# Two rows of a layer norm's gain and bias, spread over 128 partitions by TensorE in place of a broadcasting load

## The chip, the cores and the metric

The kernel runs on one core of one Trainium2 chip. The metric is device time in microseconds (us) of one execution. Names of engines: PE is TensorE (PEld its weight loads), DVE is VectorE, ACT is ScalarE, POOL is GpSimd and SP is SyncE, which here issues the weight DMAs.

## What is computed

One transformer block on 512 tokens of width 2048, all in float32. Three mixers (a spatial gating unit, a gated recurrence and latent attention) feed an output projection; then come a layer norm, a mixture of 32 experts with two experts per token, and a second layer norm. What matters here is cut down to:

```
x = layer_norm(ALPHA * x + mix, ln1_g, ln1_b)     # x: 512 x 2048
ffn = hierarchical_moe(x, ...)                    # 32 experts, top 2 of one group of 8
    # per expert e: h = silu(xb @ w_gate[e]) * (xb @ w_up[e]);  y = h @ w_down[e]
x = layer_norm(ALPHA * x + ffn, ln2_g, ln2_b)
# layer_norm: (x - mean) * rsqrt(var + eps) * g + b, g and b of length 2048
```

## The kernel before

Tokens lie in NB = 4 blocks of 128 rows. After the output projection four tiles `z[b]` (128 x 2048) hold the first norm's result without its gain and bias. For the experts these two are applied to the gathered, transposed rows, from a small column table. For the residual of the second norm they are still to be applied to `z` itself: `z = z * g + b`, where `g` and `b` must stand in every partition, since a token is a partition.

The expert loop (`for e in range(NE)`) takes the experts one after the other. For each one, `up(e)` multiplies the gathered rows by `w_gate` and `w_up` (16 chunks of 128 x 1024, 512 KB each, through the class `Ring`), and `down(e - 1)` multiplies the previous expert's hidden rows by `w_down` (8 chunks). A chunk is loaded by SP into a raw buffer (line 81), then split into a high and a low part by ACT (line 96, copy to fp32r) and DVE (line 97, subtract) into one of four pairs of buffers, and TensorE multiplies the parts (lines 1390 and 1391 in `up` where an expert has at most 64 rows, lines 156 to 158 in `down` and in `up` of larger experts). Chunks of two of the four column parts of `down` aren't split: there TensorE multiplies in plain float32 (line 1426). `Ring.done()` hands a used buffer back and pumps the next load and split. Each engine works its instructions in the order in which the program writes them, so what is written between `up(e)` and `down(e - 1)` stands there on every engine's queue.

PSUM tiles come from two rings: `acc()` with five buffers and `aux()` with three. `rows` turns the gathered rows with TensorE through `aux` (line 1348) for the next expert, `fold` and `turn_h` (lines 1400, 1407, and the split at 161 and 162) make the hidden rows of `down`.

Between `up(12)` and `down(11)` the helper `vectors` loads `ln1_g` and `ln1_b` into two tiles of 128 x 2048 (tags X7 and B2): SP issues two DMAs whose source is read 128 times, 1 MB each (line 1526). In the experts 13 to 28, between `up(e)` and `down(e - 1)`, DVE applies a quarter of one block per expert, a multiply and an add of 128 x 512 (line 1566). After the last `up`, `vectors` loads the second norm's vectors in the same way into tiles of the same tags.

Of the kernel before, what the change touches and what calls it, by code (L numbers as in the profile page):

```python
# [13 lines left out]
AF = mybir.ActivationFunctionType  # L14
# [9 lines left out]
DM = 2048  # L24
# [105 lines left out]
def build(tc, I, out):  # L130
    with ExitStack() as ctx:
        _build(tc, tc.nc, ctx, I, out)


def _build(tc, nc, ctx, I, out):
# [8 lines left out]
    def slot(tag, shape, dt=F32):  # L144
        cnt[0] += 1
        return bp.tile([P] + list(shape), dt, tag=tag, name=f"{tag}_{cnt[0]}")
# [4 lines left out]
    mm = nc.tensor.matmul  # L151
    tt, ts, stt = nc.vector.tensor_tensor, nc.vector.tensor_scalar, nc.vector.scalar_tensor_tensor
    act = nc.scalar.activation
# [73 lines left out]
    for k2 in range(8):  # L227
        t = slot(f"X{k2}", [2, 2, 512], F32R)
# [19 lines left out]
    ones = onesr.bitcast(F32)  # L248
# [28 lines left out]
    def bcast(ap, n):  # L277
        return bass.AP(tensor=ap.tensor, offset=ap.offset, ap=[[0, P], [1, n]])
# [39 lines left out]
    def acc(shape=(512,)):  # L318
        return ps.tile([P] + list(shape), F32, tag="acc", name="acc", bufs=5)

    def aux(shape=(512,)):
        return ps.tile([P] + list(shape), F32, tag="aux", name="aux", bufs=3)

    def btile():
        o = acc()
        for half in range(2):
            w = ring.get()
            for j in range(8):
                k = half * 8 + j
                c = slice(j * P, (j + 1) * P)  # L330
                mm3(o, (w[0][:, c], w[1][:, c]), xk(k), k == 0, k == KD - 1)
            ring.done()
            step()
        return o
# [114 lines left out]
    for h in range(4):  # L449
        o = btile()  # L450
# [347 lines left out]
    o = aux()  # L798
# [36 lines left out]
    def pv(h):  # L835
        o = acc()
        for s in range(NB):
            v = [x[:, s, (h % 4) * P:(h % 4 + 1) * P] for x in V[h // 4]]
            pt = [x[:, POFF[s]:POFF[s] + T - P * s] for x in ptk]
            mm3(o[:, s * P:], v, pt, s == 0, s == NB - 1)  # L840
        return o
# [55 lines left out]
    for h in range(7):  # L897
# [16 lines left out]
        o = pv(h)  # L914
# [35 lines left out]
    o = pv(7)  # L950
# [13 lines left out]
    gb1 = [slot("X7", [DM]), slot("B2", [DM])]  # L964
# [209 lines left out]
    for b in range(NB):  # L1174
        o = acc()
# [107 lines left out]
    def gates():  # L1283
        tt(gv, oh, wide(gate, [2 * NB, NE], 2), op=OP.mult)
        hl = tp[:, 0:512].rearrange("p (i a e) -> p i a e", a=2, e=NE)
        yield
        act(hl[:, :, 0], gv, AF.Copy)
        tt(hl[:, :, 1], gv, hl[:, :, 0].bitcast(F32), op=OP.subtract)
        yield
        o = aux()  # L1290
        for i in range(2 * NB):
            mm(o[:, 0:2 * NE], ohr[:, i // NB, i % NB], hl[:, i].rearrange("p a e -> p (a e)"),
               start=i == 0, stop=i == 2 * NB - 1)
        nc.vector.tensor_copy(gt, o[:, 0:NE])
        tt(gt, gt, o[:, NE:2 * NE], op=OP.add)
        yield
# [25 lines left out]
    def gather(e):  # L1322
        def move(n):
            for i in range(2):
                nc.gpsimd.indirect_dma_start(out=xgs[e % 2][0:n, H[i]], out_offset=None, in_=x1d[i][:],  # L1325
                                             in_offset=off(idx[0:n, EX[e]:EX[e] + 1]),
                                             bounds_check=T - 1, oob_is_err=False)
        if e:
            sized(e, move)
        else:  # L1330

            move(32)
            with tc.If(nc.gpsimd.value_load(cnt_i[0:1, EX[0]:EX[0] + 1]) > 32):
                move(P)
# [20 lines left out]
    def rows(e, i, *by):  # L1355

        n = 4 // len(by)
        tmp = xgs[e % 2][:, i * 512:(i + 1) * 512]
        for h, ts in enumerate(by):
            o = turn(xgs[e % 2], i, range(h * n, h * n + n))  # L1360
            for j in range(h * n, h * n + n):
                g, b = [gcol[:, a, 4 * i + j:4 * i + j + 1] for a in range(2)]
                s = slice(j * P, (j + 1) * P)
                ts(tmp[:, s], o[:, s], g, b, op0=OP.mult, op1=OP.add)
        def parts():
            d = [xT[i // 2][:, 4 * (i % 2):4 * (i % 2) + 4, :, a] for a in range(2)]
            split(d[0], d[1], tmp.rearrange("p (a t) -> p a t", t=P))
        return parts

    def up(e, hooks):  # L1370


        n = nc.tensor.value_load(cnt_i[0:1, EX[e]:EX[e] + 1])
        stt(folds[e % 2], pairs, few[:, EX[e]:EX[e] + 1], ident, op0=OP.mult, op1=OP.add)
        for which in range(2):
            o = acc()
            for c in range(8):
                if (which, c) in hooks:
                    hooks[which, c]()
                if (which, c) == (1, 2):  # L1380
                    act(raws[0], fold(e, 0), AF.Silu)
                w = ring.get()
                ks = [(2 * c + j, [v[:, j * 512:(j + 1) * 512] for v in w]) for j in range(2)]
                with tc.If(n > HALF) as more:
                    for k, wk in ks:
                        mm3(o, [xT[k // 8][:, k % 8, :, a] for a in range(2)], wk, k == 0, k == KD - 1)
                with more.Else():
                    for k, wk in ks:
                        x = xT[k // 8][:, k % 8, 0:HALF].rearrange("p t a -> p (t a)")
                        mm(o, x, wk[0], start=k == 0, stop=False)  # L1390
                        mm(o, x, wk[1], start=False, stop=k == KD - 1)  # L1391
                if c == 7:
                    act(raws[which], o, AF.Copy)
                ring.done()
# [10 lines left out]
    def turn_h(e):  # L1405
        hi, lo = [v.rearrange("p a t -> p (a t)") for v in hTs[e % 2]]
        tt(hfs[e % 2], raws[0], fold(e, 1), op=OP.mult)
        split(hi, lo, hfs[e % 2])
# [30 lines left out]
    def steps_of(e):  # L1439

        steps = {}
        for i in range(4):
            steps[(0, 2 * i + 1) if e > 1 else [(0, 5), (0, 6), (0, 7), (1, 1)][i]] = lambda i=i: later.append(rows(e, i, ts, gain_act))
            steps[1, 2 * i + 2] = lambda: later.pop(0)()
        return steps
# [73 lines left out]
    later = []  # L1519
    ring.done()  # L1520

    def vectors(*names):

        ts = [slot("X7", [DM]), slot("B2", [DM])]
        for t, name in zip(ts, names):
            nc.sync.dma_start(t, bcast(I[name], DM))
        return ts

    for e in range(NE):
        if e and e + 2 < NE:  # L1530
            gather(e + 2)
        hooks = steps_of(e + 1) if e + 1 < NE else {}
        if e == 0:
            rows(0, 1, gain_act)()
            hooks[0, 0] = lambda: later.append(rows(0, 2, ts, gain_act))

            def part3():
                later.pop()()
                later.append(rows(0, 3, ts, gain_act))
            hooks[0, 2] = part3  # L1540

            def last():
                later.pop()()
                gather(2)
            hooks[0, 4] = last
            gate_table = gates()
            for c in (0, 5, 7):
                hooks[1, c] = lambda: next(gate_table)
        if e == 1:
            hooks[0, 2] = lambda: turn_h(0)  # L1550
        up(e, hooks)
        while later:
            later.pop(0)()
        if e == 9:
            for entry in lent:
                entry[1] = True
        if e == NE - 3:
            for entry in ers:
                entry[1] = True
        if e == 12:  # L1560
            gb1 = vectors("ln1_g", "ln1_b")
        if 13 <= e < 29:

            b, s = (e - 13) // 4, slice((e - 13) % 4 * 512, ((e - 13) % 4 + 1) * 512)
            for t, op in zip(gb1, (OP.mult, OP.add)):
                tt(z[b][:, s], z[b][:, s], t[:, s], op=op)
        if e == 0:
            x4 = slot("X4", [2, 1024])
            ring.add([x4[:, 0, :]])
            hfs += [x4[:, 1, i * DE:(i + 1) * DE] for i in range(2)]  # L1570
            ring.add([misc[:, 1024:]])
            ring.pump()
        elif e < NE - 1:
            down(e - 1)
    down(NE - 2)
    lng2, lnb2 = vectors("ln2_g", "ln2_b")
    down(NE - 1)

# [151 lines left out]
```

## Time and profile before

| | us |
|---|---|
| median of 3 runs | 1927.43 (1927.27 to 1928.93) |
| the profiled execution: its own time | 1928.39 |
| its span from the first to the last instruction | 1926.6 |
| DVE busy in the span | 1415.2 (73%) |
| ACT busy in the span | 1258.6 (65%) |
| PE busy in the span (matmuls are pipelined and their ends modelled) | 1815.6 (94%) |

The expert loop fills the time from about 770 us to the end. A share of the whole span mixes it with the mixers ahead, so the loop is read from rows of its own stretches. Weight loads on PEld show best when TensorE moves on: each matmul is preceded by one, and the spacing of their starts is the pace of TensorE.

### The profile page before, as it was taken

The numbers are of one execution on the slowest core, as the hardware profiler recorded it, in microseconds if no ns is written. First come the engines' busy times: TensorE is split into PE (matmuls) and PEld (weight loads), VectorE is DVE, ScalarE is ACT, GpSimd is POOL, SyncE is SP. The second block draws the span as 40 slices with busy tenths as digits, with TensorE's granted clock in tenths as the row PEclk, the third lists the DMA queues.
The fourth block names the chain that finished last, engine by engine and source line by source line (L and its number), as shares of the span: only waits on it lengthen the run. The fifth ranks groups of instructions, "written<-read, shape, count | busy, mean of one in ns | idle before, by whom it ended". The sixth has DMA issues, their size and how long they took to land.

```text
span 1926.6 us, 25404 instructions
## 1 busy us (share of the span) xinstructions
PE 1815.6 (94%) x8235; PEld 1366.7 (71%) x8236; DVE 1415.2 (73%) x2041; ACT 1258.6 (65%) x1758; POOL 242.0 (13%) x192
## 2 busy tenths in 40 slices
PE   9999999999999997899999999999999999999990
PEld 7888888887887896666666666666766666667650
DVE  5656433467564446988989889898898998988866
ACT  4533363635452224888878888787887878878862
POOL 1000000010000001112112121211212212121010
PEclk9999999999999997999999999999999999999995
DMA  7222222223145225899999999999999999999895
GB/s 252 98 88 77 77 68 97 98 88 131 44 166 193 92 82 193 290 352 381 391 392 383 390 337 393 395 378 390 383 364 395 392 393 378 381 388 385 294 348 184
DMA packets 142574, 510.78 MB, mean 265 GB/s; under 512 B 18625, under 2 KB 18673, under 8 KB 141361
## 3 DMA queue, kind: packets, MB, share of 16 engines
q1 hardware_dynamic: 131040, 477.16, 65.9%
q0 software_dynamic: 10768, 29.74, 5.7%
q8 instruction: 93, 1.52, 0.3%
q10 hardware_dynamic: 576, 1.57, 0.2%
q14 instruction: 97, 0.79, 0.1%
HBM read 488.53 MB, written 22.02 MB: 265 GB/s over the span
## 4 chain that ended last, share of the span: by engine, by line
issue 48%; POOL 5%; DMA 2%; DVE 2%; POOLq 1%; ACT 0%; PE 0%; DVEq 0%; ACTq 0%
POOL yd L1338 2%; DMA yd<-M,idx 2%; POOL M L1325 2%; POOL B L1325 2%; POOLq L1310 1%; DVE B L1620 0%; DVE X L1616 0%; POOLq L1316 0%; DVE whl L97 0%; DMA X<-w_up 0%; DVE B L1625 0%; DMA B<-yd 0%; ACT whl L96 0%; DVE B L162 0%; POOLq L1338 0%
## 5 line engine op out<-in xcount | busy, mean ns | idle before, releaser
L97 DVE TENSOR_TENSOR whl<-X,whl 128x1024 fp32r<-128x1024 f32 x312 | 377.5, 1221 | 97.4 <-ACT whl L96 67.8
L97 DVE TENSOR_TENSOR whl<-wraw,whl 128x1024 fp32r<-128x1024 f32 (+1 forms) x222 | 269.8, 1218 | 226.6 <-ACT whl L96 211.8
L96 ACT ACTIVATE whl<-wraw 128x1024 fp32r<-128x1024 f32 (+1 forms) x222 | 235.0, 1062 | 220.6 <-PE acc L157 94.0
L96 ACT ACTIVATE whl<-X 128x1024 fp32r<-128x1024 f32 x312 | 330.2, 1072 | 61.2 <-PE acc L158 39.6
L1391 PE MATMUL acc<-whl,B 128*128 128x512 f32 x696 | 287.0, 412 | 15.4 <-DVE whl L97 15.3
L1390 PE MATMUL acc<-whl,B 128*128 128x512 f32 x696 | 293.4, 421 | 2.1 <-ACT whl L96 1.7
L1338 POOL DMA_INDIRECT yd<-M,idx x64 | 90.4, 1412 | 871.6 <-ACT M L1430 866.1
L1391 PEld LDWEIGHTS acc<-whl,B 128*128 128x128 f32 x696 | 131.2, 188 | 86.7 <-DVE whl L97 59.5
L158 PE MATMUL acc<-whl,B 128*128 128x512 f32 (+1 forms) x480 | 181.4, 378 | 0.0
L157 PE MATMUL acc<-whl,B 128*128 128x512 f32 (+1 forms) x424 | 165.8, 391 | 14.6 <-DVE whl L97 14.6
L156 PE MATMUL acc<-whl,B 128*128 128x512 f32 (+1 forms) x424 | 179.2, 423 | 0.1
L1390 PEld LDWEIGHTS acc<-whl,B 128*128 128x128 f32 x696 | 131.3, 189 | 32.0 <-issue 4.8
L156 PE MATMUL acc<-X,whl 128*128 128x512 f32 x384 | 151.0, 393 | 0.0
L157 PE MATMUL acc<-X,whl 128*128 128x512 f32 x384 | 149.6, 390 | 0.3 <-DVE X L162 0.3
L158 PE MATMUL acc<-X,whl 128*128 128x512 f32 x384 | 149.6, 390 | 0.0
L1426 PE MATMUL acc<-X,X 128*128 128x512 f32 x308 | 141.2, 592 | 0.0
L97 DVE TENSOR_TENSOR X<-X,X 128x1024 fp32r<-128x1024 f32 x105 | 128.1, 1220 | 17.2 <-ACT X L96 12.9
L96 ACT ACTIVATE X<-X 128x1024 fp32r<-128x1024 f32 x105 | 112.4, 1070 | 19.8 <-PE acc L158 14.9
L1430 ACT ACTIVATE M<-acc,X 128x512 f32<-128x512 f32 x128 | 87.2, 681 | 50.3 <-PE acc L1426 43.7
L157 PEld LDWEIGHTS acc<-whl,B 128*128 128x128 f32 x424 | 80.5, 190 | 47.7 <-DVE whl L97 26.9
L1391 PE MATMUL acc<-X,B 128*128 128x512 f32 x232 | 97.8, 421 | 10.0 <-DVE X L97 9.9
L158 PEld LDWEIGHTS acc<-whl,B 128*128 128x128 f32 x480 | 90.9, 189 | 15.7
(451 smaller groups left out, 3596.0 us busy)
## 6 DMA issues: line engine op xcount, KB each, us to landing
X<-w_down SPq DMA_DIRECT2D x169, 512.0 KB
X<-w_gate SPq DMA_DIRECT2D x160, 512.0 KB
X<-w_up SPq DMA_DIRECT2D x160, 512.0 KB
wraw<-w_gate SPq DMA_DIRECT2D x69, 512.0 KB
wraw<-w_up SPq DMA_DIRECT2D x69, 512.0 KB
wraw<-w_in SPq DMA_DIRECT2D x64, 512.0 KB
wraw<-w_down SPq DMA_DIRECT2D x64, 512.0 KB
B<-w_up SPq DMA_DIRECT2D x27, 512.0 KB
```

The costliest lines, as they stand in the source:

```text
L96: nc.scalar.activation(h[:, s], r[:, s], AF.Copy)
L97: nc.vector.tensor_tensor(l[:, s], r[:, s], h[:, s].bitcast(F32), op=OP.subtract)
L156: mm(o, a[0], b[0], start=start, stop=False)
L157: mm(o, a[0], b[1], start=False, stop=False)
L158: mm(o, a[1], b[0], start=False, stop=stop)
L1310: n = nc.gpsimd.value_load(cnt_i[0:1, EX[e]:EX[e] + 1])
L1325: nc.gpsimd.indirect_dma_start(out=xgs[e % 2][0:n, H[i]], out_offset=None, in_=x1d[i][:], in_offset=off(idx[0:n, EX[e]:EX[e] + 1]), bounds ...
L1338: nc.gpsimd.indirect_dma_start(out=yd[i][:], out_offset=off(index), in_=y[:, H[i]], in_offset=None, bounds_check=T - 1, oob_is_err=False, ...
L1390: mm(o, x, wk[0], start=k == 0, stop=False)
L1391: mm(o, x, wk[1], start=False, stop=k == KD - 1)
L1426: mm(o, hfs[e % 2][:, k * P:(k + 1) * P], w[:, cs], start=k == 0, stop=k == 3)
L1430: act(yts[-1][:, n * 512:(n + 1) * 512], o, AF.Copy, scale=gt[:, EX[e]:EX[e] + 1])
```

## The change

The load of `ln1_g` and `ln1_b` between `up(12)` and `down(11)` becomes two DMAs of one row each (1 x 2048, 8 KB) into partition 0 of the same tiles. In the experts 13 and 14, between `up(e)` and `down(e - 1)`, a new helper `spread` makes each quarter of the tiles whole: a float32 matmul of a row of ones (1 x 128) with a quarter row (1 x 512) gives 128 equal rows in an `aux` tile, and ACT copies them into the tile. Each of the two experts does four of these: two quarters of each vector. The 16 pairs of DVE operations on `z` move two experts later, to the experts 15 to 30. The second norm's vectors are loaded as before.

```
+    def spread(t, q):
+
+        o, s = aux(), slice(q * 512, (q + 1) * 512)
+        mm(o, ones[0:1], t[0:1, s], start=True, stop=True)
+        act(t[:, s], o, AF.Copy)
...
         if e == 12:
-            gb1 = vectors("ln1_g", "ln1_b")
-        if 13 <= e < 29:
-
-            b, s = (e - 13) // 4, slice((e - 13) % 4 * 512, ((e - 13) % 4 + 1) * 512)
+            gb1 = [slot("X7", [DM]), slot("B2", [DM])]
+            for t, name in zip(gb1, ("ln1_g", "ln1_b")):
+                nc.sync.dma_start(t[0:1], I[name])
+        if 13 <= e < 15:
+            for q in (2 * e - 26, 2 * e - 25):
+                for t in gb1:
+                    spread(t, q)
+        if 15 <= e < 31:
+
+            b, s = (e - 15) // 4, slice((e - 15) % 4 * 512, ((e - 15) % 4 + 1) * 512)
             for t, op in zip(gb1, (OP.mult, OP.add)):
                 tt(z[b][:, s], z[b][:, s], t[:, s], op=op)
```

On TensorE, at the end of `up(13)` (whl is a split chunk, X_119 and B_120 are the two vectors' tiles):

```order
 L1391 MATMUL acc<-whl,B_116_6158 128x512
 L1384 UNCONDITIONAL_BRANCH
+L1525 MATMUL aux<-X_119_12008,onesr 128x512
+L1525 MATMUL aux<-B_120_12009,onesr 128x512
+L1525 MATMUL aux<-X_119_12008,onesr 128x512
+L1525 MATMUL aux<-B_120_12009,onesr 128x512
 L156 MATMUL acc<-whl,B_111_5475 128x512
 L157 MATMUL acc<-whl,B_111_5475 128x512
```

Four matmuls stand between the last one of `up(13)` and the first one of `down(12)`; the same four stand once more behind `up(14)`.

On ACT, at the same place (whl and X_96 are halves of chunk pairs, M_118 is a result of `down`):

```order
 L96 ACTIVATE whl<-B_106_5386 128x1024
 L161 ACTIVATE B_116_6158<-M_108_5395 128x512
+L1526 ACTIVATE X_119_12008<-aux 128x512
+L1526 ACTIVATE B_120_12009<-aux 128x512
+L1526 ACTIVATE X_119_12008<-aux 128x512
+L1526 ACTIVATE B_120_12009<-aux 128x512
 L96 ACTIVATE whl<-wraw 128x1024
 L1430 ACTIVATE M_118_6918<-acc,X_101_3986 128x512
```

The four copies stand behind two splits that were there before, the last of them line 161, and ahead of the split at line 96 with which the next chunk begins.

On SP, in the stream of weight loads behind `up(12)`:

```order
 L81 DMA wraw<-w_up 128x1024
 L81 DMA X_101_3986<-w_up 128x1024
-L1526 DMA X_119_12008<-ln_g 128x2048
-L1526 DMA B_120_12009<-ln_b 128x2048
+L1569 DMA X_119_12008<-ln_g 1x2048
+L1569 DMA B_120_12009<-ln_b 1x2048
 L81 DMA X_99_3984<-w_up 128x1024
 L81 DMA wraw<-w_up 128x1024
```

The two issues keep their place; only their size differs.

## Rows read from the trace of the kernel before

**Rows 1.** The profile page: busy time, and DMA in 40 slices.

```profile
PE 1815.6 (94%) x8235; PEld 1366.7 (71%) x8236; DVE 1415.2 (73%) x2041; ACT 1258.6 (65%) x1758; POOL 242.0 (13%) x192
...
DMA  7222222223145225899999999999999999999895
```

**Rows 2.** Busy time by stretch, one expert each, from end of down to end.

```profile
core 0: us, PE busy (x) PEld busy (x) DVE busy (x) ACT busy (x) POOL busy (x), PEclk, DMA share, GB/s
1178.30:1212.35 34.05, 32.60 (x137) 22.38 (x136) 29.49 (x36) 28.72 (x40) 6.78 (x4) 1.00 1.03 395
1212.35:1246.41 34.06, 32.62 (x138) 22.41 (x137) 30.09 (x37) 28.44 (x40) 5.83 (x4) 1.00 1.03 392
1246.41:1280.50 34.09, 32.61 (x138) 22.37 (x137) 30.79 (x37) 28.69 (x41) 6.94 (x4) 1.00 1.03 393
1280.50:1314.88 34.38, 32.90 (x138) 22.40 (x137) 30.71 (x37) 28.49 (x41) 5.97 (x4) 1.00 1.03 377
1110.17:1144.27 34.10, 32.62 (x138) 22.38 (x137) 29.50 (x36) 28.80 (x40) 6.90 (x4) 1.00 0.96 327
```

**Rows 3.** Line 1526's DMAs, then line 1566: min/median/max ns, first and last start.

```profile
L1526 SPq DMA_DIRECT2D X<-ln_g x2: 424/424/424, 1204.4 to 1868.7; - x2
...
L1566 DVE TENSOR_TENSOR B<-B,X x16: 677/688/693, 1238.6 to 1754.1; 128x512 f32<-128x512 f32 x16
```

**Rows 4.** Timeline, PEld, end of up(13), then down(12): start, us, instruction, [idle].

```profile
1232.97 0.19 PEld L156 LDWEIGHTS acc<-whl,B 128*128 128x128 f32 x1
1234.14 0.19 PEld L157 LDWEIGHTS acc<-whl,B 128*128 128x128 f32 x1 [0.98 <-DVE whl L97]
...
1237.55 0.30 PEld L1426 LDWEIGHTS acc<-wraw,X 128*128 128x128 f32 x2
1238.09 0.19 PEld L1426 LDWEIGHTS acc<-wraw,X 128*128 128x128 f32 x1 [0.24 <-issue]
...
1240.67 0.19 PEld L156 LDWEIGHTS acc<-whl,B 128*128 128x128 f32 x1 [0.24 <-issue]
...
1246.41 0.19 PEld L1426 LDWEIGHTS acc<-X,X 128*128 128x128 f32 x1 [0.24 <-issue]
```

**Rows 5.** Timeline, ACT, around the same place.

```profile
1232.45 0.71 ACT L161 ACTIVATE B<-M 128x512 fp32r<-128x512 f32 x1
1233.00 1.08 ACT L96 ACTIVATE whl<-X 128x1024 fp32r<-128x1024 f32 x1
...
1235.37 0.71 ACT L161 ACTIVATE B<-M 128x512 fp32r<-128x512 f32 x1
1236.38 1.06 ACT L96 ACTIVATE whl<-wraw 128x1024 fp32r<-128x1024 f32 x1 [0.30 <-DMA wraw<-w_gate]
```

**Rows 6.** Line 1430, ACT copies out of PSUM: min/median/max ns.

```profile
L1430 ACT ACTIVATE M<-acc,X x128: 667/687/692, 828.5 to 1883.1; 128x512 f32<-128x512 f32 x128
```

**Rows 7.** Timeline around the start of up(13): PEld, ACT, then DVE.

```profile
1213.67 0.19 PEld L1391 LDWEIGHTS acc<-whl,B 128*128 128x128 f32 x1
...
1214.38 1.06 ACT L96 ACTIVATE whl<-X 128x1024 fp32r<-128x1024 f32 x1 [0.28 <-DMA B<-ln_b]
...
1211.64 1.23 DVE L97 TENSOR_TENSOR whl<-X,whl 128x1024 fp32r<-128x1024 f32 x1 [0.66 <-ACT whl L96]
...
1215.47 1.23 DVE L97 TENSOR_TENSOR whl<-X,whl 128x1024 fp32r<-128x1024 f32 x1 [2.34 <-issue]
```

**Rows 8.** Who PEld and ACT waited for, 1212.35 to 1246.41: us, times, longest.

```profile
PEld acc L1391 <- DVE whl L97: 2.1, 4, 1.0
PEld acc L1391 <- DVE X L97: 1.2, 2, 0.8
PEld acc L157 <- DVE whl L97: 1.0, 1, 1.0
...
ACT B L161 <- DVE X L1407: 4.0, 1, 4.0
```

## The prediction

> **What bounds the kernel now.** I began with the page's busy shares and its DMA line [rows 1]. They suggest two bounds for the expert loop at once: PE at 94% and DMA at 9 tenths or more for most of the second half. Neither says which wait ends last, so I cut the loop into experts, from the end of one `down` on TensorE (the last weight load of line 1426, as at 1246.41 [rows 4]) to the next, and read each stretch [rows 2]. Three things are to be seen there. An expert with few rows takes 34.05 us. It takes the same with no work on `z` (the stretch from 1178.30) as with it (from 1212.35 on, where DVE is busier by 0.6 to 1.3 us). And it takes 34.10 where the DMA rate fell to 327 GB/s (from 1110.17), against 395 GB/s elsewhere. So a share of 1.03 doesn't mean that DMA sets the pace: the loads follow the buffers that the engines hand back.
>
> What sets the pace is seen where `up` passes into `down`, and back. In `down` TensorE runs without a stall: its plain float32 matmuls of 512 columns take two weight loads at 0.43 us each (1238.09 to 1240.67 is six steps in 2.58 us), so 0.86 us a matmul; the 0.24 us named there is part of that step [rows 4]. Meanwhile ACT and DVE run ahead until all four chunk pairs are split. ACT's next split, at 1214.38, starts only when TensorE has used the first chunk of `up(13)`, whose last weight load starts at 1213.67, and DVE stands idle for 2.34 us before it [rows 7]. So each `up` starts with a full stock, and whatever ACT and DVE could do beyond it is lost. In `up` TensorE eats the stock and ends by waiting for DVE's subtractions: 2.1 + 1.2 + 1.0 us of weight-load waits in this expert, all on line 97 [rows 8].
>
> **The change, part by part.**
>
> *The load.* Two DMAs of 1 MB each, issued from 1204.4 [rows 3], become two of 8 KB. At 392 GB/s [rows 2] the 2.10 MB are 5.3 us of transfer. What they cost the loop is read from the experts behind them: 34.06, 34.09 and 34.38 us against 34.05, so 0.01 + 0.04 + 0.33 = **0.4 us** [rows 2]. Those I give back. ACT's wait of 0.28 us behind `ln_b` [rows 7] lies in the first of these. SP issues as many DMAs as before, in the same places. A row of 8 KB on one partition has no row in this trace; it has the whole of `up(13)` to land, over 20 us, while the 1 MB forms were past by 1214.38, 10 us after their issue.
>
> *The four matmuls per spread expert.* TensorE would start `down(12)` at 1232.97 and is free to. Its second matmul, line 157, in fact starts at 1234.14, because DVE's part of the chunk comes late; a step without a wait is 0.23 us, so 0.94 us of this is waiting [rows 4]. No row shows a float32 matmul with a single row of weights. The nearest is line 1426: the same 512 columns and type with 128 rows, 0.86 us. I take that, since what streams past is the same 512 columns; below it, a quarter of it (0.23 us, the fp32r step in the same rows) is the floor.
>
> The Trainium skill (TensorE: Matmul & The Clock Gate, section on why this matters for your kernels) says that a matmul over 32 rows takes the time of one over 128, which speaks for the value I take. The same page (section on the back-to-back issue gap) gives N/2.4 + 2.5 ns, or 216 ns for 512 columns: by that the four would take 0.86 us, where line 1426's rows say 3.44 us. The rows decide.
>
> The tiles come from `aux`, which has three buffers. So the fourth matmul waits for ACT's first copy, and ACT is late here: in its order the first copy stands behind the split at line 161, which starts at 1235.37, and the next ACT instruction can follow 0.55 us after such a start (1232.45 to 1233.00) [rows 5]. A copy of 128x512 out of PSUM takes 0.69 us [rows 6]. Step by step: matmuls 1 to 3 run from 1232.97 to 1235.55; the first copy from 1235.92 to 1236.61; matmul 4 to 1237.47; line 157 starts 0.23 us on, at 1237.70, instead of 1234.14. That is **3.56 us later**, once in each of the two experts: 7.1 us. The bounds for one expert: with no wait for the copy, 3.44 + 0.23 - 1.17 = 2.5 us; with the wait but nothing gained from the old stall, 3.56 + 0.94 = 4.5 us. With the floor price only the copy would count: 1236.61 + 0.23 + 0.23 - 1234.14 = 2.9 us, so the price of the matmul matters less than the ring.
>
> Nothing behind it takes this back. `down` runs at TensorE's own pace, and the next `up` starts with the same four pairs as before.
>
> *The copies on ACT.* Four at some 0.6 us, 2.4 us, are put ahead of the split that started at 1236.38 [rows 5]. That split makes stock for the next `up`, over 8 us away on TensorE and now 3.6 us later; and ACT waits 4.0 us in this same `down` for line 1407 [rows 8]. So I cost them at nothing beyond the wait above. If that cover were gone, up to 2.4 us in each expert would be added.
>
> *The work on `z`.* 16 pairs of 0.69 us leave the experts 13 and 14 and come in 29 and 30. An expert with them takes as long as one without [rows 2], so both ends cost nothing; DVE's 2.34 us of idle time [rows 7] covers the 1.4 us. The tiles are needed again by the load for the second norm, issued at 1868.7; the last pair, at 1754.1 now [rows 3], would come two experts later, near 1830. That load doesn't wait for it.
>
> **The sum.** 7.1 - 0.4 = +6.7 us on the profiled execution's 1928.39 us, 1935.1 us. Its own time stands 0.96 us above the median of 1927.43, so the median should come to **1934.1 us**, 0.35% slower. A difference of 0.2%, 3.9 us, is about what a measurement here can tell from none.
>
> **The rivals.**
>
> *The loop is bound by its transfers.* Then 2.09 MB less is 5.3 us less, and TensorE's extra work goes into its waits: 1927.4 - 5.3 = 1922.1 us. For it stands the share of 1.03 in every expert. The Trainium skill (Perfetto Trace Analysis, on the most-contended engine) calls DMA occupancy misleading, because there are 16 engines; the trace agrees. Against it stand the flat 34.05 to 34.10 us at 327 and at 395 GB/s. It would decide if the stretches after the load had grown by 5 us in sum; they grew by 0.4. Chance 4%.
>
> *The four matmuls hide in TensorE's waits.* It waits some 4.3 us per expert for DVE [rows 8]; if DVE used the stop of 3.5 us to get ahead for good, only the 0.4 us would be seen: about 1927 us, no change. The stop lies at the one place that could help, the end of `up`. It decides if the stock of pairs isn't full when the next `up` starts. Against it: DVE's idle 2.34 us at that start says that it is. Chance 10%.
>
> *More than forecast.* The two experts' copies also delay a split that `down` needs, or the old stall isn't gained: 2 x 4.5 - 0.4 = 8.6 us or more, 1936 us and above. For it: ACT's queue is full there. Against: the first chunk that `down` multiplies is already split on ACT by then. Chance 8%.
>
> The forecast, 1931.9 to 1936 (2 x 2.5 - 0.4 = 4.6 us at its lower end), has the other 78%. The range of 1930.3 to 1936.6 takes in its bounds, a little of partial hiding below, and the near end of the last rival. **Chances:** slower by over 0.2%: 78 + 8 - 2 (the part of the forecast that partial hiding takes below 1931.3) = 84%; within 0.2%: 10 + 2 = 12%; faster: 4%.
>
> **What would show it.** In the profile after, eight matmuls at line 1525 with two weight loads each, 0.43 us apart; the fourth of each set starting after the first copy at line 1526. The experts 13 and 14 (end of `down` to end of `down`) at about 37.6 us, the next ones at 34.05, and the 34.38 gone. DMA busy near 1210 carries 2 MB less with no gain of its own. I am wrong if these two experts keep 34.05 us (the stop is hidden), if later experts run shorter than 34.05 (TensorE wasn't the pace), or if the fourth matmul doesn't wait (then the sum falls to 4.6 us).

## The result and the profile after

The changed kernel takes 1941.80 us (median of 4 runs, 1940.45 to 1942.39) against 1928.18 us of the kernel before, measured beside it: a ratio of 1.0065, with a 95% interval of 1.0054 to 1.0077 (the two medians alone make 1.0071). It is slower, as forecast, but by 13.6 us where 6.7 were expected, and outside the range of 1930.3 to 1936.6 us.

The trace after, cut from end of `down` to end of `down` as in [rows 2] (the same columns):

```profile
core 0: us, PE busy (x) PEld busy (x) DVE busy (x) ACT busy (x) POOL busy (x), PEclk, DMA share, GB/s
1178.47:1212.53 34.06, 32.62 (x138) 22.40 (x137) 29.48 (x36) 28.75 (x40) 5.63 (x4) 1.00 1.02 393
1212.53:1253.52 40.99, 39.61 (x145) 25.63 (x144) 29.66 (x36) 31.15 (x44) 5.83 (x4) 0.92 0.93 335
1253.52:1294.52 41.00, 39.59 (x146) 25.62 (x145) 29.67 (x36) 31.14 (x44) 6.95 (x4) 0.92 0.90 319
1294.52:1328.60 34.08, 32.62 (x138) 22.37 (x137) 30.07 (x37) 28.46 (x40) 5.68 (x4) 1.00 1.01 351
```

The whole loss lies in the two experts that spread the vectors: 6.9 us each over 34.05. The experts next to them take what they took before, but for expert 15, whose 34.38 us are now 34.08. The forecast had 37.6 us for each of the two. The column PEclk tells what else is in them: 0.92, where every expert of [rows 2] had 1.00. Cut finer, with the stretches at the lower level on their own:

```profile
1212.53:1237.21 24.68, 23.30 (x98) 15.53 (x97) 22.33 (x29) 23.34 (x35) 4.36 (x3) 1.00 1.02 376
1237.21:1244.04 6.83, 6.83 (x16) 4.46 (x15) 2.88 (x3) 2.25 (x5) 0.00 (x0) 0.50 0.82 324
1244.04:1253.52 9.48, 9.48 (x34) 5.64 (x34) 4.45 (x5) 5.56 (x7) 1.47 (x1) 1.00 0.75 235
1278.17:1285.00 6.83, 6.83 (x16) 4.41 (x15) 2.92 (x3) 2.23 (x5) 0.00 (x0) 0.50 0.74 295
```

For 6.83 us in each of the two, TensorE was granted half its clock, 1.2 GHz instead of 2.4. Where that falls is seen on the weight loads, at the place of [rows 4]:

```profile
1232.91 0.19 PEld L1391 LDWEIGHTS acc<-whl,B 128*128 128x128 f32 x1
1233.47 0.29 PEld L1525 LDWEIGHTS aux<-X,onesr 1*128 1x128 f32 x2 [0.37 <-DMA X<-w_gate]
...
1234.86 0.18 PEld L1525 LDWEIGHTS aux<-X,onesr 1*128 1x128 f32 x1 [0.24 <-PE aux L1525]
1235.29 0.18 PEld L1525 LDWEIGHTS aux<-X,onesr 1*128 1x128 f32 x1 [0.24 <-issue]
1236.80 0.29 PEld L1525 LDWEIGHTS aux<-B,onesr 1*128 1x128 f32 x2 [1.32 <-ACT X L1526]
1238.43 0.29 PEld L156 LDWEIGHTS acc<-whl,B 128*128 128x128 f32 x1 [1.34 <-issue]
1238.60 0.34 PEld L157 LDWEIGHTS acc<-whl,B 128*128 128x128 f32 x1
1239.03 0.33 PEld L158 LDWEIGHTS acc<-whl,B 128*128 128x128 f32 x1
...
1243.30 1.44 PEld L1400 LDWEIGHTS aux<-R,B 128*128 128x128 f32 x8
```

The four matmuls stand as forecast: loads 0.43 us apart, and 1.32 us without a load ahead of the fourth, which waits for the first copy (0.24 us of such a gap is part of the step). But then the loads of lines 157 and 158 stand 0.43 us apart. In the kernel before, the same step took 0.23 us:

```profile
1234.48 0.19 PEld L156 LDWEIGHTS acc<-whl,B 128*128 128x128 f32 x1
1234.71 0.19 PEld L157 LDWEIGHTS acc<-whl,B 128*128 128x128 f32 x1
```

From 1238.60 to 1243.30, eleven steps take 4.70 us instead of 2.5. The rest of the loss at half clock is in the fourth matmul and in the first loads of line 1400. ACT meanwhile does what the forecast said, and then waits (compare [rows 5]):

```profile
1235.56 0.72 ACT L161 ACTIVATE B<-M 128x512 fp32r<-128x512 f32 x1
1236.12 0.63 ACT L1526 ACTIVATE X<-aux 128x512 f32<-128x512 f32 x1
...
1238.54 0.60 ACT L1526 ACTIVATE B<-aux 128x512 f32<-128x512 f32 x1 [0.82 <-PE aux L1525]
1241.40 1.06 ACT L96 ACTIVATE whl<-wraw 128x1024 fp32r<-128x1024 f32 x1 [2.26 <-DMA X<-w_up]
```

Two questions follow. Is the half clock the cause of the other 3.4 us per expert? And what brought it about: that these matmuls fill one row of the array, that TensorE's weight loads stood still for 1.3 us, or something on ACT?

### The profile page after: what moved, and what is told of

The parts are those of the page before. It is cut to its first block, busy times and chain, and to the rows that moved or that the text cites. A ratio compares the mean times of both kernels' runs of the same rounds, so it can differ in the third digit from the quotient of the medians.

```text
span 1940.4 us, 25444 instructions
## 1 busy us (share of the span) xinstructions
PE 1828.8 (94%) x8251; PEld 1372.9 (71%) x8252; DVE 1413.9 (73%) x2041; ACT 1263.0 (65%) x1766; POOL 236.2 (12%) x192
## 4 chain that ended last, share of the span: by engine, by line
issue 49%; POOL 5%; DVE 2%; DMA 2%; POOLq 2%; ACT 0%; DVEq 0%; ACTq 0%
POOL yd L1338 2%; POOL B L1325 1%; POOL M L1325 1%; DMA yd<-M,idx 1%; POOLq L1310 1%; DVE B L1632 0%; POOLq L1316 0%; DVE X L1628 0%; DVE whl L97 0%; DMA X<-w_up 0%; DVE B L1637 0%; DMA B<-yd 0%; DVE B L162 0%; POOLq L1338 0%; DVE X L97 0%
## 5 line engine op out<-in xcount | busy, mean ns | idle before, releaser
L157 PE MATMUL acc<-whl,B 128*128 128x512 f32 (+1 forms) x424 | 166.4, 392 | 13.6 <-DVE whl L97 13.5
```

The lines of the kernel that those rows point to most:

```text
L157: mm(o, a[0], b[1], start=False, stop=False)
```

## The experiments

Each edit is against the changed kernel, and the times are medians beside runs of the kernel before. The ratios aren't formed from the two medians and differ from theirs by up to 0.0008.

| run | this, us | before, us | ratio, 95% interval |
|---|---|---|---|
| full rows, whole load | 1940.64 | 1928.65 | 1.0054, 1.0037 to 1.0071 |
| the same kernel again | 1936.55 | 1929.21 | 1.0033, 1.0022 to 1.0044 |
| zeroed tiles, 128 rows | 1936.12 | 1928.65 | 1.0036, 1.0023 to 1.0049 |
| one row, no wait | 1940.44 | 1928.65 | 1.0063, 1.0046 to 1.0079 |
| 128 rows, no wait | 1934.31 | 1928.65 | 1.0029, 1.0020 to 1.0039 |
| 32 rows | 1941.85 | 1929.21 | 1.0063, 1.0044 to 1.0082 |
| one row, two per expert | 1936.64 | 1929.21 | 1.0039, 1.0025 to 1.0053 |
| one row, one per expert | 1932.89 | 1929.21 | 1.0018, 1.0009 to 1.0026 |
| 128 rows, one per expert | 1929.97 | 1929.40 | 1.0002, 0.9993 to 1.0011 |

**Full rows, the whole load.** The same four matmuls, buffers, wait and copies, but with all 128 rows.

```
-        mm(o, ones[0:1], t[0:1, s], start=True, stop=True)
+        mm(o, ident, t[:, s], start=True, stop=True)
...
-            gb1 = [slot("X7", [DM]), slot("B2", [DM])]
-            for t, name in zip(gb1, ("ln1_g", "ln1_b")):
-                nc.sync.dma_start(t[0:1], I[name])
+            gb1 = vectors("ln1_g", "ln1_b")
```

> The vectors are loaded whole, as before the change, and the four matmuls per expert multiply a 128 x 128 identity with 128 x 512 of the tile, so all 128 rows take part; the place, the three aux buffers, the copies and the moved work on z stay as in the changed kernel. Theory 'clock' (matmuls of one row don't hold TensorE's clock, and 3.4 us per expert are lost at half clock): the granted clock stays at 1.00 in the experts 13 and 14, which take 37.6 us each; +7.1 us on the kernel before, about 1935.3 us. Rival 'stall' (the clock falls because TensorE stands still for the fourth aux tile): the clock falls to 0.5 as in the changed kernel, 41 us per expert, about 1941.8 us. Rival 'copies' (ACT's copies delay splits): about 1941.8 us too, without regard to the clock.

The kernel was run a second time:

> The run with full rows and the whole load once more, the same kernel. Its profile had the expert loop as the theory 'clock' said, but 6.4 us more than the kernel before ahead of the loop, where the two have the same instructions. If that loss belongs to single executions, the time comes to about 7.1 us over the kernel before, near 1935.7 us; if it belongs to the kernel, near 1940.6 us again.

In the second run, busy time by expert, and then the weight loads at the place of the change:

```profile
1213.14:1250.79 37.65, 36.06 (x145) 23.90 (x144) 29.67 (x36) 31.17 (x44) 6.97 (x4) 1.00 1.03 392
1250.79:1288.43 37.64, 36.03 (x145) 23.88 (x144) 29.67 (x36) 31.17 (x44) 5.80 (x4) 1.00 1.00 369
1288.43:1322.49 34.06, 32.62 (x138) 22.40 (x137) 30.07 (x37) 28.41 (x40) 5.68 (x4) 1.00 1.01 355
```

```profile
1235.71 0.19 PEld L1525 LDWEIGHTS aux<-X,identr 128*128 128x128 f32 x1 [0.24 <-issue]
1237.43 0.30 PEld L1525 LDWEIGHTS aux<-B,identr 128*128 128x128 f32 x2 [1.53 <-ACT X L1526]
1237.97 0.19 PEld L156 LDWEIGHTS acc<-whl,B 128*128 128x128 f32 x1 [0.24 <-issue]
1238.39 0.19 PEld L157 LDWEIGHTS acc<-whl,B 128*128 128x128 f32 x1 [0.24 <-issue]
1238.63 0.19 PEld L158 LDWEIGHTS acc<-whl,B 128*128 128x128 f32 x1
```

The clock stays at 1.00, though TensorE's weight loads stand still even longer ahead of the fourth matmul, 1.53 us; lines 157 and 158 go on at 0.23 us (1238.39 and 1238.63). The two experts take 3.6 us more, the forecast's 3.56. So the rival "stall" falls, and so does the rival "copies": the copies are all there. The mean granted clock of whole executions agrees with the one trace of each kernel: 0.979 or 0.980 in the four of the changed kernel, 0.982 or 0.983 in the eight of this run. By the medians the second run lost 7.3 us. The first run's median lost 12.0; its expert loop reads the same (37.63 us for expert 13, clock 1.00), but its profile has a stretch of half clock ahead of the loop, where no instruction differs:

```profile
448.79:462.44 13.65, 13.65 (x42) 10.43 (x43) 7.21 (x17) 5.39 (x12) 0.00 (x0) 0.50 0.31 126
```

The kernel before and the second run had 1.00 there. The profiled execution of the next run, with zeroed tiles, has such a stretch too, from 448.56 to 458.80 us, and took 1941.62 us against that run's median of 1936.12; so it isn't the full data's own. Why an execution falls to half clock there stayed open; single totals can carry some 5 us of it, and the loop is therefore read from its own rows.

**Zeroed tiles, 128 rows.** One row is loaded, but the other 127 are zeros and take part.

```
+                nc.gpsimd.memset(t, 0.0)
                 nc.sync.dma_start(t[0:1], I[name])
...
-        mm(o, ones[0:1], t[0:1, s], start=True, stop=True)
+        mm(o, ones, t[:, s], start=True, stop=True)
```

> One row per vector is loaded as in the changed kernel, but GpSimd zeroes the tiles first and the matmuls take all 128 rows (127 of them zero) against 128 x 128 ones. Theory 'clock', if rows count whatever they hold: clock 1.00, experts 13 and 14 at 37.6 us, 7.1 - 0.4 = +6.7 us, about 1934.9 us. If what the rows hold counts: the clock falls and the time is that of the changed kernel, 1941.8 us. Rivals 'stall' and 'copies': 1941.8 us. The difference to the run with full rows and the whole load is the price of that load: 0.4 us by the forecast.

```profile
1218.12:1255.74 37.62, 36.05 (x146) 23.89 (x145) 29.66 (x36) 31.13 (x44) 6.96 (x4) 1.00 0.99 363
1255.74:1293.38 37.64, 36.05 (x145) 23.89 (x144) 29.65 (x36) 31.16 (x44) 5.81 (x4) 1.00 0.97 346
1293.38:1327.42 34.04, 32.60 (x137) 22.39 (x136) 30.07 (x37) 28.30 (x40) 5.69 (x4) 1.00 1.02 361
```

The same as with full data: what the 127 rows hold doesn't matter, only that they take part. This run is the change as the forecast had costed it, and it lost 7.5 us by the medians against 6.7. Against the second run with the whole load, its two experts differ by under 0.05 us, and expert 15 behind them takes 34.04 us here and 34.06 there: ahead of such a stop the whole load cost nothing.

**One row, no wait.** The fourth tile comes from the five `acc` buffers.

```
-    def spread(t, q):
+    def spread(t, q, tile=aux):
 
-        o, s = aux(), slice(q * 512, (q + 1) * 512)
+        o, s = tile(), slice(q * 512, (q + 1) * 512)
...
-                    spread(t, q)
+                    spread(t, q, acc if q % 2 and t is gb1[1] else aux)
```

> The changed kernel, but the fourth tile of each set comes from the five acc buffers, so that no matmul waits for a copy; the matmuls still have one row. Rival 'stall': the clock stays at 1.00, 2 x 2.5 - 0.4 = +4.7 us, about 1932.9 us. Theory 'clock': the clock falls again if a stretch of 3.4 us of one-row matmuls is long enough for it, then 2 x (2.5 + 3.4) - 0.4 = +11.4 us, about 1939.6 us; if it stays, the length of the stretch decides, and this run alone can't tell theory from rival. Rival 'copies': 1941.8 us less at most 2 x 1.0.

The two experts, and their stretches at the lower level:

```profile
1212.96:1251.61 38.65, 37.75 (x146) 24.88 (x145) 29.67 (x36) 31.03 (x44) 5.82 (x4) 0.96 0.97 351
1251.61:1291.92 40.31, 39.42 (x145) 25.47 (x144) 29.66 (x36) 31.16 (x44) 5.80 (x4) 0.92 0.91 326
1237.31:1240.73 3.42, 3.42 (x8) 2.47 (x8) 1.99 (x3) 1.38 (x4) 0.00 (x0) 0.50 1.03 405
1274.86:1281.69 6.83, 6.83 (x14) 3.94 (x13) 3.30 (x5) 3.60 (x6) 0.00 (x0) 0.50 0.95 372
```

No matmul waits for a copy, and the clock falls all the same, for 3.42 us in one expert and 6.83 us in the other.

**128 rows, no wait.** Zeroed tiles and the fourth tile from `acc`, both edits above together.

> Zeroed tiles and 128 rows, and the fourth tile from acc: neither one-row matmuls nor the wait for a copy. Theory 'clock': clock 1.00, the experts 13 and 14 at 34.05 + 2.5 = 36.6 us, +4.7 us, about 1932.9 us; against the run with zeroed rows and the wait this gives the price of the wait alone, 2 x 1.0 us. Rival 'stall': the same. Rival 'copies': near 1940 us.

```profile
1213.47:1250.12 36.65, 35.72 (x146) 23.98 (x145) 29.68 (x36) 31.07 (x44) 6.96 (x4) 1.00 1.00 368
1250.12:1286.78 36.66, 35.76 (x145) 23.97 (x144) 29.66 (x36) 31.05 (x44) 5.80 (x4) 1.00 0.99 358
```

2.6 us per expert, the forecast's lower bound of 2.5. The wait for a buffer to come back is thus worth 37.63 - 36.65 = 1.0 us per expert. These two rows also price the clock in the run before this one: with half of 3.42 and of 6.83 us on top they make 38.4 and 40.1 us, and 38.65 and 40.31 were measured. The medians lost 5.7 us, 1.0 more than expected.

**32 rows.** The tiles' first 32 rows zeroed, and 32 rows in the matmuls; the wait stays.

```
+                nc.gpsimd.memset(t[0:32], 0.0)
...
-        mm(o, ones[0:1], t[0:1, s], start=True, stop=True)
+        mm(o, ones[0:32], t[0:32, s], start=True, stop=True)
```

> As the run with zeroed rows, with 32 rows in the matmuls instead of 128; wait for the fourth tile as in the changed kernel. Theory 'clock': more rows than one, fewer than all; if a quarter of the rows holds the clock, the experts 13 and 14 take 37.6 us at 1.00 (+6.7 us in all); if it doesn't, 41 us at 0.5 for a part of them (+13.6 us in all). Rival 'stall' fell already with the runs before; no other theory tells rows apart.

```profile
1212.61:1251.97 39.36, 37.97 (x145) 24.86 (x144) 29.66 (x36) 31.13 (x44) 5.82 (x4) 0.96 0.94 348
1251.97:1292.77 40.80, 39.40 (x146) 25.40 (x145) 29.68 (x36) 31.14 (x44) 6.93 (x4) 0.92 0.89 318
1238.27:1241.69 3.42, 3.42 (x10) 2.64 (x9) 0.70 (x3) 1.40 (x2) 0.00 (x0) 0.50 1.01 400
1275.82:1282.65 6.83, 6.42 (x12) 3.96 (x13) 2.86 (x4) 2.99 (x5) 0.00 (x0) 0.50 0.89 347
```

A quarter of the rows doesn't hold the clock either. These rows also give the sum: 0.50 was granted for 3.42 us in the first expert and 6.83 us in the second. Half of each, 1.7 and 3.4 us, with the 3.6 us of the full-row runs on 34.05 us makes 39.35 and 41.05 us; measured are 39.36 and 40.80.

**One row, two per expert, then one per expert.** The spreads go to the experts 13 to 16, or 13 to 20, and `z` is worked quarter by quarter.

```
-        if 13 <= e < 15:
-            for q in (2 * e - 26, 2 * e - 25):
-                for t in gb1:
-                    spread(t, q)
...
+        if 13 <= e < 17:
+            for t in gb1:
+                spread(t, e - 13)
...
```

> One-row matmuls as in the changed kernel, but two per expert (one quarter of both vectors) in the experts 13 to 16, and the work on z taken quarter by quarter from expert 14 on. No matmul waits for a copy; the one-row stretch is 1.7 us instead of 5. Theory 'clock': nearly all of TensorE's time around the stretch is full-row work, so the clock stays at 1.00 and each of the four experts takes 34.05 + 1.72 + 0.23 - 1.17 = 34.83 us; 4 x 0.78 - 0.3 = +2.8 us. If even this stretch drops the clock, up to 3.4 us more per expert, +16 us. Rival 'copies' (two copies per expert cost time on ACT): the experts longer than 34.83 us at a clock of 1.00.

```profile
1212.53:1247.87 35.34, 34.43 (x141) 23.06 (x140) 29.57 (x36) 29.95 (x42) 6.96 (x4) 1.00 1.02 384
1247.87:1283.23 35.36, 34.46 (x141) 23.03 (x140) 30.78 (x38) 29.75 (x42) 6.95 (x4) 1.00 0.98 354
1283.23:1320.19 36.96, 36.06 (x141) 24.17 (x140) 30.87 (x38) 30.07 (x42) 5.69 (x4) 0.95 1.03 374
```

Twice the clock held and twice it fell (the fourth expert reads like the third): with the same instructions on TensorE it can go either way. And even at 1.00 an expert takes 35.35 us where I expected 34.83.

```
+        if 13 <= e < 21:
+            spread(gb1[(e - 13) % 2], (e - 13) // 2)
...
```

> One one-row matmul per expert, in the experts 13 to 20, and the work on z quarter by quarter from expert 15 on. TensorE's stall before line 157 is 0.94 us and the matmul takes 0.86 us, so by the sum of the forecast it is hidden whole: 34.05 us per expert, clock 1.00, -0.3 us on the kernel before, which is no measurable difference. If the stall doesn't cover it: up to 8 x 0.86 = +6.9 us.

Its first expert, and the weight loads of the spread there:

```profile
1213.92:1248.44 34.52, 33.62 (x140) 22.67 (x138) 29.49 (x36) 29.28 (x41) 5.83 (x4) 1.00 1.02 386
```

```profile
1234.31 0.19 PEld L1391 LDWEIGHTS acc<-whl,B 128*128 128x128 f32 x1
1234.86 0.29 PEld L1525 LDWEIGHTS aux<-X,onesr 1*128 1x128 f32 x2 [0.36 <-DMA X<-w_gate]
1235.91 0.19 PEld L156 LDWEIGHTS acc<-whl,B 128*128 128x128 f32 x1 [0.76 <-ACT whl L96]
```

The clock held in all eight experts, yet 0.45 us are lost in each of seven, and 1.3 us in expert 17, the one large expert among them (39.59 us against 38.28; the next expectation counts it twice). The loads tell where: the spread's first load stands 0.55 us behind the one before it, and the load after the spread 0.94 us behind its second, which starts 0.11 us after the first, at 1234.97. The last run shows what these are with full rows.

**128 rows, one per expert.** As before, with zeroed tiles and `ones` whole.

> As the run with one one-row matmul per expert, but with zeroed tiles and 128 rows. That run lost 0.45 us in each of its eight experts (twice 1.3 us where the expert has many rows and no stall), though the clock stayed at 1.00. If the loss is the one-row form's (its weight load starts late, and the one behind it waits for its end), the eight experts take 34.05 us here, but for 0.9 us in the two parts of the large expert without a stall; with the third of a microsecond that expert 15 gives back, -0.3 + 0.9 = +0.6 us, no measurable difference. If TensorE's stall is smaller than its weight loads show (0.55 us instead of 0.94), about 0.3 us per expert stay, +2.4 us and more. Rival 'copies': the same 0.45 us per expert as with one row.

The weight loads at the same place, and two of the eight experts:

```profile
1233.63 0.19 PEld L1391 LDWEIGHTS acc<-whl,B 128*128 128x128 f32 x1
1233.86 0.42 PEld L1525 LDWEIGHTS aux<-X,onesr 128*128 128x128 f32 x2
1234.53 0.19 PEld L156 LDWEIGHTS acc<-whl,B 128*128 128x128 f32 x1 [0.24 <-issue]
1235.03 0.19 PEld L157 LDWEIGHTS acc<-whl,B 128*128 128x128 f32 x1 [0.32 <-DVE whl L97]
```

```profile
1213.24:1247.36 34.12, 33.20 (x139) 22.81 (x138) 29.49 (x36) 29.24 (x41) 6.97 (x4) 1.00 1.02 385
1281.46:1315.57 34.11, 33.19 (x140) 22.82 (x139) 30.09 (x37) 28.81 (x41) 6.82 (x4) 1.00 1.03 375
```

Here the first load follows after 0.23 us, the one behind the spread 0.44 us after the second load (1234.09), and line 157 still waits a little for DVE: the matmul fits into TensorE's old stall, and an expert with it takes 34.08 to 34.12 us. The time is that of the kernel before (ratio 1.0002). It doesn't beat it: the load that it saves is worth the 0.3 us of expert 15 (34.38 in [rows 2], 34.11 here), too little to measure, and the large expert 17, which has no such stall, takes 0.9 us more (39.22 against 38.28).

## Why the prediction was wrong

**What held.** TensorE's pace and not the transfers bounds the loop: no expert after the two is shorter than 34.02 us. The load's price was about right: expert 15 gives back 0.3 us of the 0.4 in the sum. The changed kernel alone doesn't show that this is the load's, since expert 15 gave it back with the whole load ahead of the stop too; the last run, which has neither the load nor the stop, bears it out (34.11 us). The work on `z` costs nothing in the experts 29 and 30 (38.29 and 34.02 us, 38.29 and 34.06 before), and the four copies cost nothing beyond the wait. A one-row matmul's two loads take 0.43 us each, as taken from line 1426, though its ends cost something besides (0.45 us an expert with one of them), which the sum didn't have. The fourth matmul waits for the first copy, worth 1.0 us per expert. And 3.56 us per expert is what the same steps cost with full rows, 3.6 us, where the clock stays at 1.00.

**The step that failed** is "Nothing behind it takes this back. `down` runs at TensorE's own pace". Nothing took it back, but the pace itself changed. I carried the 0.23 us step of [rows 4] over to the matmuls behind the spread, and so left a term out of the sum: the granted clock. It fell to 0.50 for 6.83 us in each of the two experts. Half of that is 3.4 us, and 3.6 + 3.4 = 7.0 us against the measured 6.94. Two experts make 6.8 us of the 6.9 by which the loss of 13.6 passed the forecast of 6.7. The row of the clock was before my eyes, 1.00 in every expert, and I took it for a property of the loop, which the new matmuls would leave alone.

The three kernels with 128 rows at that place and the one with one full-row matmul per expert kept 1.00; those with one or 32 rows, four at a time, fell in both experts, without a wait (one row) as with it. Two one-row matmuls fell in two of four experts, one in none of eight. The clock's part is thus shown by taking the rows away and giving them back. The Trainium skill (TensorE: Matmul & The Clock Gate, section on the HAM clock gate) says that the clock is set by how busy TensorE has been. The runs agree in so far as the run with zeroed tiles kept 1.00 and the one with 32 rows fell, and the two differ in nothing but how many rows are zeroed and multiplied. They show besides that four matmuls over 1 or 32 rows, with loads 0.43 us apart, didn't hold the clock where four over 128 rows at the same pace did, whatever the rows held. Why the rows count, and why two thin matmuls lose the clock in one expert and not in another, no run shows.

**The rivals.** The transfer-bound loop and the hidden matmuls fell as the forecast weighed them. "More than forecast" names 1936 us and above, and the result lies there, but by luck: it counts on a delayed split or on an old stall that isn't gained, 4.5 us per expert or more, and with full rows, where both could have shown, an expert loses 3.6 us. The clock isn't among its causes.

## What to carry to other kernels

A small matmul put into a stream of full ones can cost more than its own duration: look at which rows it fills, since here four thin ones in a row halved the clock for what stood behind them. Give such a spread all 128 rows (zeros will do), place it where TensorE waits anyway, and count the PSUM buffers: the fourth of four on a ring of three waited for an evacuation, 1.0 us here. And before saving a transfer, read what it costs the loop: here 2.1 MB at a DMA share of 1.03 were worth 0.3 us, which didn't show in the total.

## What the hardware showed that I had not expected

Four float32 matmuls of one row brought the granted clock from 1.00 to 0.50 for 6.83 us in each of two experts; 32 rows did so too, for 3.42 and 6.83 us; 128 rows of which 127 were zero did not, and neither did 1.53 us without a weight load between full-row matmuls. A one-row matmul's first weight load, and the load behind its second, come later than those of full rows: after 0.55 and 0.94 us where full rows show 0.23 and 0.44, and an expert with one such matmul lost 0.45 us. The last expert took 0.3 to 1.1 us less in the changed kernels than the 35.47 us before, but the time from its end to the end of the kernel grew by 0.5 to 1.2 us (by 0.85 in the changed kernel, whose last expert took 0.65 less), so this isn't a gain.
